# A pooled input half by seven products behind the state-space branch, and half the pooled parts kept on chip

## The chip, the cores and the metric

The kernel runs on one core of a Trainium2 chip, as one launch. The metric is device time in microseconds (us), taken over repeated runs; lower is better. The engines are named as in the profile: PE is TensorE (matmuls), PEld its weight loads, DVE is VectorE, ACT is ScalarE, POOL is GpSimd, SP is SyncE. SP issues the weight loads; POOL issues the transfers spoken of here.

## The reference

One layer of a decoder trunk on 512 tokens of width 1024, in float32. After a modulated RMS norm, one input product gives the inputs of three branches and three gates. The branches are a state-space one (SSD), dilated attention, and pooling over four windows:

```python
    for gi, w in enumerate(POOL_WINDOWS):        # 2, 4, 8, 16
        csg = cs[:, :, gi]
        shifted = jnp.pad(csg, ((0, 0), (w, 0), (0, 0)))[:, :S]
        count = jnp.minimum(t + 1, w).astype(jnp.float32)[None, :, None]
        outs.append((csg - shifted) / count - ug[:, :, gi])
    pooled = jnp.stack(outs, axis=2)
    return jnp.einsum('bsgi,gio->bsgo', pooled, w_mix).reshape(b, S, POOL_WIDTH)
...
    y_pool = (_multi_scale_pool(u.astype(f32), w_pool_mix) * pool_scale).astype(dtype) @ w_pool_out
...
    return (g_ssd * y_ssd + g_attn * y_attn + g_pool * y_pool) @ w_out
```

`u` has 1024 channels in four groups of 256, one for each window, and `w_mix` is one 256 x 256 matrix for each group. Behind the output product come a residual, a second modulated norm, and a feed-forward layer (1024 to 4096 with a squared ReLU, and back).

## The kernel before, in words

**Data.** Activations lie with the channels on the 128 partitions and the 512 tokens along a row, in blocks of 128 x 512. Blocks come from one pool of numbered slots: `blk(name)` takes a free slot, `free` gives it back, and the next taker waits until all that read or wrote the slot has ended. Eight PSUM banks work alike (`acc`, `psm`).

**Products.** A float32 product is made of three matmuls (`mm3`, L304 to L307): each operand is split into a high part (rounded) and a low part (the rest), and high x low, high x high and low x high are added up in PSUM. `gemm_feat` (L309) makes a half (512 outputs) as four banks, over 8 rows of weights; that is 96 matmuls of 512 columns. The weights come through `wstream` (L291), two rows at a time: SP loads `raw`, ACT makes the high part `wh` (a cast, L288), DVE the low part `wl` (L288). In the mode `st["adds"]`, ACT makes minus the high part (L281) and a DMA issued by POOL adds the weights from DRAM to it (L282), so that DVE has nothing to do for the weights. Three `wh` and three `wl` tiles are in turn, so a cast waits for the matmuls that used the tile three steps before.

**Seven products.** `seven_products` (L781) makes the same half by Strassen's scheme: seven products of quarter size in place of eight, with sums of quarters of the weights (`wsum`, made on DVE, L808 to L811) and of the input (`tx`, `ty`, made once by `input_sums`, L763, and used by all later calls). These are 168 matmuls of 256 columns (L826); their casts stand at L801 and L802, and the results are put together on DVE (L838).

**Branches.** The pooled branch: `pool(half)` makes four blocks of `u`, then on DVE the window sums (copies of 1 to 8 columns and adds of the shifted block, L1131 and L1132), the edge factors (L1136), the mean less `u` (L1137), and splits the result into `pdh` and `pdl` (L333). `pool_mix(gi)` multiplies one group by its matrix: two banks of 6 matmuls, each evacuated by ACT (L1167, high part) and DVE (L1168, low part) into two of eight staging blocks; a DMA on POOL (L1172) stores each part in DRAM. Later `again` (L1292) loads all 16 parts back.

**Order.** The program's text gives the order, and a scheduler arranges instructions by priority within it. `call` puts work on a side list, and after each pair of weight rows `tick` (L261) issues the next entry of it behind that pair's casts. Around the change the order before was: U's first half, U's second half (from here in the mode `adds`), the first gate of the state-space branch (GS 0) with the mixing of all four groups and the four pieces of the input sums on the side list, the first projection of that branch, GS 1 by seven products (the mode `adds` off), the second projection; then the reloads, the first pooled gate (GP 0) by seven products, its projection (which reads the pooled parts), GP 1, its projection, the output product.

**Output section.** The output product's second half is made in halves of 256 tokens (`out_block`, L1349, `ta` and `tb`), so that sums over tokens of squares (`sum_tokens`, L1366) and the second norm's factor (`spread`, L216) can be made for the first half while the second is still multiplied; `ff_rows` does the first feed-forward block by halves as well.

## Time and profile before

| what | value |
|---|---|
| time, median of 3 runs | 1091.45 us (1090.39 to 1092.57) |
| the profiled execution's own time | 1090.45 us |
| span of its trace | 1088.7 us |
| granted TensorE clock, mean | 1.0 |
| PE / DVE / ACT / POOL busy, share of the span | 99% / 69% / 50% / 4% |
| DMA, mean over the span | 137 GB/s |

The profiled execution lies 1.0 us under the median of the runs. The span goes from its first instruction to its last, and the time has 1.75 us around it. In a row of a timeline the first number is the start, the second the duration of one row, `x2` means two instructions in a row, and the bracket tells how long the engine was idle before and what ended that. Matmuls are pipelined: a 512-column matmul shows 0.39 us, and the next starts earlier than that, so prices are read from start to start. The same holds for DVE, whose durations overlap by some 0.08 us.

### The profile page before, as it was taken

The numbers are of one execution on the slowest core, as the hardware profiler recorded it, in microseconds if no ns is written. First come the engines' busy times: TensorE is split into PE (matmuls) and PEld (weight loads), VectorE is DVE, ScalarE is ACT, GpSimd is POOL, SyncE is SP. The second block draws the span as 40 slices with busy tenths as digits, with TensorE's granted clock in tenths as the row PEclk, the third lists the DMA queues.
The fourth block names the chain that finished last, engine by engine and source line by source line (L and its number), as shares of the span: only waits on it lengthen the run. The fifth ranks groups of instructions, "written<-read, shape, count | busy, mean of one in ns | idle before, by whom it ended". The sixth has DMA issues, their size and how long they took to land.

```text
span 1088.7 us, 15639 instructions
## 1 busy us (share of the span) xinstructions
PE 1081.3 (99%) x6022; PEld 934.0 (86%) x6022; DVE 748.1 (69%) x1429; ACT 547.6 (50%) x889; POOL 39.8 (4%) x70
## 2 busy tenths in 40 slices
PE   8999999999999999999999999999999999999998
PEld 7878888888887888888879989899889989989987
DVE  8955746684677966567966556667878587587664
ACT  8965874543444943757554335354434334335330
POOL 0000000000000010001311100000000000000000
PEclk9999999999999999999999999999999999999999
DMA  9723143546555243247956534450215224134032
GB/s 352 298 97 92 64 162 121 194 155 200 176 179 152 98 137 114 78 116 176 266 178 203 142 120 141 132 211 1 97 39 156 80 75 145 60 106 137 20 116 78
DMA packets 50958, 148.71 MB, mean 137 GB/s; under 512 B 6066, under 2 KB 6834, under 8 KB 50884
## 3 DMA queue, kind: packets, MB, share of 16 engines
q1 hardware_dynamic: 43088, 126.08, 34.7%
q0 software_dynamic: 7072, 20.45, 7.6%
q8 instruction: 47, 0.77, 0.3%
q10 hardware_dynamic: 724, 1.18, 0.3%
q14 instruction: 27, 0.22, 0.1%
HBM read 141.37 MB, written 6.32 MB: 136 GB/s over the span
## 4 chain that ended last, share of the span: by engine, by line
PE 96%; DVE 2%; DMA 1%; ACT 1%; issue 1%; SPq 0%; DVEq 0%; ACTq 0%
PE psacc L305 22%; PE psacc L307 22%; PE psacc L306 22%; PE psacc L826 17%; PE psacc L545 4%; PE psS L624 1%; PE psy L1087 1%; PE pso L740 1%; PE psyo L1095 1%; PE pso L738 1%; DMA rawl<-in_w_in_dram 1%; PE psqT L603 0%; PE pskT L608 0%; PE psst L1046 0%; PE pspT L721 0%
## 5 line engine op out<-in xcount | busy, mean ns | idle before, releaser
L288 DVE TENSOR_TENSOR wl<-raw,wh 128x1024 fp32r<-128x1024 f32 x116 | 141.6, 1222 | 126.1 <-ACT wh L288 116.4
L288 ACT CAST wh<-raw 128x1024 fp32r<-128x1024 f32 x116 | 121.5, 1049 | 185.6 <-PE psacc L306 105.6
L305 PE MATMUL psacc<-hl,wh 128*128 128x512 f32 x320 | 128.8, 403 | 0.2 <-ACT pT L722 0.2
L307 PE MATMUL psacc<-hh,wl 128*128 128x512 f32 x320 | 124.7, 390 | 0.0
L306 PE MATMUL psacc<-hh,wh 128*128 128x512 f32 x320 | 124.6, 389 | 0.0
L306 PE MATMUL psacc<-ah,wh 128*128 128x512 f32 (+1 forms) x260 | 100.4, 386 | 0.0
L305 PE MATMUL psacc<-al,wh 128*128 128x512 f32 (+1 forms) x260 | 100.4, 386 | 0.0
L307 PE MATMUL psacc<-ah,wl 128*128 128x512 f32 (+1 forms) x260 | 100.3, 386 | 0.0
L305 PE MATMUL psacc<-wl,rh 128*128 128x512 f32 x192 | 77.4, 403 | 0.0
L307 PE MATMUL psacc<-wh,rl 128*128 128x512 f32 x192 | 75.2, 392 | 0.0
L306 PE MATMUL psacc<-wh,rh 128*128 128x512 f32 x192 | 75.1, 391 | 0.0
L305 PEld LDWEIGHTS psacc<-hl,wh 128*128 128x128 f32 x320 | 60.1, 188 | 13.4 <-issue 1.2
L306 PEld LDWEIGHTS psacc<-hh,wh 128*128 128x128 f32 x320 | 60.2, 188 | 13.3 <-issue 1.4
L307 PEld LDWEIGHTS psacc<-hh,wl 128*128 128x128 f32 x320 | 60.0, 188 | 12.9
L1470 DVE SCALAR_TENSOR_TENSOR xr<-psacc,modv,xr 128x512 f32<-128x512 f32 (+1 forms) x65 | 44.7, 739 | 20.4 <-PE psacc L307 20.4
L802 DVE TENSOR_TENSOR wl<-rawl,wh 128x512 fp32r<-128x512 f32 (+1 forms) x36 | 33.6, 954 | 35.4 <-ACT wh L801 35.3
L307 PEld LDWEIGHTS psacc<-ah,wl 128*128 128x128 f32 x260 | 48.8, 188 | 9.8
L305 PEld LDWEIGHTS psacc<-al,wh 128*128 128x128 f32 x260 | 48.9, 188 | 9.7
L306 PEld LDWEIGHTS psacc<-ah,wh 128*128 128x128 f32 x260 | 48.9, 188 | 9.6
L801 ACT CAST wh<-wsum 128x1024 fp32r<-128x1024 f32 x18 | 19.0, 1054 | 75.7 <-PE psacc L306 73.8
L801 ACT CAST wh<-rawl 128x512 fp32r<-128x512 f32 (+1 forms) x36 | 29.1, 833 | 49.8 <-PE psacc L306 25.1
L305 PEld LDWEIGHTS psacc<-wl,rh 128*128 128x128 f32 x192 | 36.1, 188 | 7.7 <-ACT qT L604 0.5
(426 smaller groups left out, 2777.9 us busy)
## 6 DMA issues: line engine op xcount, KB each, us to landing
raw<-in_w_in_dram SPq DMA_DIRECT2D x74, 512.0 KB, 3.6
raw<-in_w_ff_dram SPq DMA_DIRECT2D x52, 512.0 KB, 3.7
wa<-in_w_ada_dram SPq DMA_DIRECT2D x64, 256.0 KB, 3.4
wada<-in_w_ada_dram SPq DMA_DIRECT2D x14, 512.0 KB, 7.9
rawl<-in_w_ff_dram SPq DMA_DIRECT2D x12, 512.0 KB, 3.5
wst<-in_w_in_dram SPq DMA_DIRECT2D x16, 256.0 KB, 7.9
M<-prow POOLq DMA_DIRECT2D x16, 256.0 KB, 3.7
wl<-in_w_in_dram POOLq DMA_DIRECT2D x8, 512.0 KB, 5.5
```

What stands on the lines that cost most here:

```text
L288: edges[:] = S.copy(wh, raw), V.tensor_tensor(wl, raw, wh.bitcast(F32), ALU.subtract)
L305: mm(ps, lhsT=wh, rhs=xl, start=first, stop=False)
L306: mm(ps, lhsT=wh, rhs=xh, start=False, stop=False)
L307: mm(ps, lhsT=wl, rhs=xh, start=False, stop=last)
L545: mm(ps[j], lhsT=t[:, j, :], rhs=w, start=first, stop=last)
L624: mm(so[b], lhsT=qT[:, b * P : (b + 1) * P], rhs=kT[:, (b + 1) * P - n : (b + 1) * P], start=True, stop=True)
L738: mm(od, lhsT=vs[kb][:, hs], rhs=pT[b // 2][:, cs : cs + P], start=(b == 0), stop=False, skip_group_check=True)
L740: mm(ov[:, b, :], lhsT=vs[b][:, hs], rhs=pT[0][:, b * P : (b + 1) * P], start=False, stop=(gi == 2 and b == 3), skip_group_check=True)
L801: S.copy(h, x)
L802: V.tensor_tensor(l, x, h.bitcast(F32), ALU.subtract)
L826: mm(o, lhsT=x[:, cs], rhs=y, start=first and k == 0 and j == 0 and n == 0, stop=k == 3 and n == 2, skip_group_check=True)
L1470: V.scalar_tensor_tensor(xT[d][:, ts], p[:, : ts.stop - ts.start], modv[:, 3, d : d + 1], xT[d][:, ts], ALU.mult, ALU.add)
```

## The change

The order becomes: U's first half as before; GS 0 (now the first in the mode `adds`) and the first state-space projection with the mixing of groups 0 and 1 on the side list, and the input sums issued behind the gate's last evacuation; GS 1 by seven products; the second projection; **then U's second half, by seven products**; GP 0 by seven products with the mixing of groups 2 and 3 on its side list; the reloads; the pooled projections with GP 1 between them. Only groups 0 and 1 go to DRAM and back (8 stores, 8 reloads); groups 2 and 3 are written straight into blocks that the projection reads. The matrices of groups 2 and 3 are split into ordinary blocks. The eight staging blocks are given back after group 1.

In the output section the first block is made for all 512 tokens at once, the sums over tokens and the norm's factor are issued amid a later block's matmuls, and the first feed-forward block does rows 0 to 4 by halves and rows 5 to 7 for all tokens, into the same four banks; its squared ReLU then takes 512 columns at once.

```diff
@@ -1120,8 +1120,7 @@
             yl.append(l)
 
 
-    def pool(half):
-        us = evac(gemm_feat(w_in, 8, U + half, hh, hl), "u")
+    def pool(half, us):
         for j in range(4):
             gi = 2 * half + j // 2
             u = us[j]
@@ -1141,17 +1140,22 @@
             dh.append(x)
             dl.append(y)
 
-    mixw, stage = [], []
+    mixw, mixp, stage = [], [], []
 
     def mix_weights(n):
 
         raw = raws.tile([P, 2, T], F32, tag="raw", name=uid("wmix"))
         for i in range(2):
             nc.sync.dma_start(raw[:, i, :].rearrange("p (k c) -> p k c", k=2), a["w_pool_mix"][2 * n + i])
-        wh, wl = (exp.tile([P, 2, T], F32R, tag=f"{x}{n}", name=uid("wm" + x)) for x in "LN")
-        S.copy(wh, raw)
-        V.tensor_tensor(wl, raw, wh.bitcast(F32), ALU.subtract)
-        mixw.extend([t[:, i, :].rearrange("p (k c) -> p k c", k=2) for t in (wh, wl)] for i in range(2))
+        if n == 0:
+            wh, wl = (exp.tile([P, 2, T], F32R, tag=f"{x}{n}", name=uid("wm" + x)) for x in "LN")
+            S.copy(wh, raw)
+            V.tensor_tensor(wl, raw, wh.bitcast(F32), ALU.subtract)
+            parts = [(wh[:, i, :], wl[:, i, :]) for i in range(2)]
+        else:
+            parts = [split(raw[:, i, :], "wm") for i in range(2)]
+            mixp.extend(parts)
+        mixw.extend([t.rearrange("p (k c) -> p k c", k=2) for t in p] for p in parts)
 
     def pool_mix(gi):
         wh, wl = mixw[gi]
@@ -1163,15 +1167,21 @@
             cs = slice(m * P, (m + 1) * P)
             for k in range(2):
                 mm3(ps, wh[:, k, cs], wl[:, k, cs], dh[2 * gi + k], dl[2 * gi + k], k == 0, k == 1)
-            x, y = stage[4 * (gi % 2) + 2 * m : 4 * (gi % 2) + 2 * m + 2]
+            if gi < 2:
+                x, y = stage[4 * gi + 2 * m : 4 * gi + 2 * m + 2]
+            else:
+                x, y = blk("poolh", F32R), blk("pooll", F32R)
             S.activation(x, ps, AF.Copy, scale=vc("pool_scale", gi * 2 + m))
             V.scalar_tensor_tensor(y, ps, vc("pool_scale", gi * 2 + m), x.bitcast(F32), ALU.mult, ALU.subtract)
             free(ps)
             for t, l in ((x, ph_), (y, pl_)):
-                l.append(dp.tile([P, T], F32, name=uid("pool")))
-                nc.gpsimd.dma_start(l[-1], t.bitcast(F32))
-        if gi == 3:
+                l.append(t if gi > 1 else dp.tile([P, T], F32, name=uid("pool")))
+                if gi < 2:
+                    nc.gpsimd.dma_start(l[-1], t.bitcast(F32))
+        if gi == 1:
             free(*stage)
+        elif gi > 1:
+            free(*mixp[gi - 2])
         free(*dh[2 * gi : 2 * gi + 2], *dl[2 * gi : 2 * gi + 2])
 
 
@@ -1208,6 +1218,14 @@
 
     def take_z(g):
         return evac(gemm_feat(w_in, 8, Z + g, hh, hl), "z", AF.Silu)
+
+    def behind_evac(f):
+
+        def go():
+            with tc.issue_after(st["evac"].ins):
+                f()
+
+        return go
 
     def rest(n):
         side.extend([lambda: None] * n)
@@ -1270,32 +1288,31 @@
     show("oT", [h.bitcast(F32) for h in oh + ol])
     tq, sums = input_sums(hh, hl)
 
-    pool(0)
+    pool(0, evac(gemm_feat(w_in, 8, U, hh, hl), "u"))
     call(mix_weights, 0)
     st["adds"] = True
-    pool(1)
+    sg = gate(GS, 0)
     call(pool_mix, 0)
-    side.append(lambda: (mix_weights(1), pool_mix(1)))
-    call(pool_mix, 2)
-    call(pool_mix, 3)
-    side.extend(sums)
-    sg = gate(GS, 0)
+    call(pool_mix, 1)
+    side.extend(behind_evac(f) for f in sums)
     project(a["w_ssd_out"], 8, 0, yh, yl, sg)
     flush()
     st["adds"] = False
     sg = gate(GS, 1, tq)
     project(a["w_ssd_out"], 8, 1, yh, yl, sg)
-
-    def again(l, name):
-        for i, d in enumerate(l):
-            l[i] = blk(name, F32R)
+    pool(1, seven_products(w_in, U + 1, hh, hl, tq))
+    call(mix_weights, 1)
+    call(pool_mix, 2)
+    call(pool_mix, 3)
+    sg = gate(GP, 0, tq)
+    flush()
+    for l, name in ((ph_, "poolh"), (pl_, "pooll")):
+        for i in range(4):
+            d, l[i] = l[i], blk(name, F32R)
             nc.gpsimd.dma_start(l[i], d)
-
-    again(ph_, "poolh")
-    again(pl_, "pooll")
-    for ch in range(2):
-        sg = gate(GP, ch, tq, ch == 1)
-        project(a["w_pool_out"], 8, ch, ph_, pl_, sg, last=True)
+    project(a["w_pool_out"], 8, 0, ph_, pl_, sg, last=True)
+    sg = gate(GP, 1, tq, True)
+    project(a["w_pool_out"], 8, 1, ph_, pl_, sg, last=True)
     flush()
     assert not background
     show("mixed", [h.bitcast(F32) for h in mh + ml])
@@ ...
-        for j in range(4):
+        both = slice(0, T)
+        residual(both, 0, out_block(both, 0))
+        for j in range(1, 4):
             sq = residual(ta, j, out_block(ta, j))
...
+        ps = out_block(tb, 1, 3, lambda: rs.append(scale(sum_tokens(ta, sq))))
         residual(tb, 1, ps)
+        ps = out_block(tb, 2, 5, lambda: rs.append(spread(rs[0], 2, "r2")))
...
+        ff_rows(ta, (0,))
         sp = sum_tokens(tb, sq)
...
+        ff_rows(ta, (3, 4))
...
+        ff_rows(tb, range(5))
...
+        ff_rows(both, range(5, 8))
...
-    square_relu(0, [[(ffa[j], ta), (ffb[j], tb)] for j in range(4)])
+    square_relu(0, [[(ff[j], full)] for j in range(4)])
```

In the rows of order below, a name's number tells tiles of one name apart. First VectorE at the start of GS 1. Before, all input sums (`tx`, `ty`, from `tq`) are made when the weights of the first products (`wl`, L802) come:

```order
L333 TENSOR_TENSOR txl_5298<-tq_5154,txh_5297 128x512
L333 TENSOR_TENSOR tyl_5302<-tq_5155,tyh_5301 128x512
L802 TENSOR_TENSOR wl_5322<-rawl_5313,wh_5321 128x512
L802 TENSOR_TENSOR wl_5322<-rawl_5317,wh_5321 128x512
L811 TENSOR_TENSOR rawl_5313<-raw_5314,wsum_5327 128x2x256
L811 TENSOR_TENSOR rawl_5317<-raw_5318,wsum_5332 128x2x256
L802 TENSOR_TENSOR wl_5370<-raw_5314,wh_5369 128x512
L802 TENSOR_TENSOR wl_5370<-raw_5318,wh_5369 128x512
L907 TENSOR_TENSOR sg_5109<-psacc_5117,sg_5109 128x512
L907 TENSOR_TENSOR sg_5110<-psacc_5118,sg_5110 128x512
L914 TENSOR_TENSOR sg_3936<-sg_3936,sg_5109 128x512
L907 TENSOR_TENSOR sg_5111<-psacc_5119,sg_5111 128x512
```

Now the last pooled low part to be stored (`pool_4838`, L1175) stands just ahead, and the input sums of later pieces stand between it and the weights; `txl_5031` and `tyl_5035` take staging blocks that hold stored parts:

```order
L1175 SCALAR_TENSOR_TENSOR pool_4838<-psmix_4909,vec_79,pool_4837 128x512
L767 TENSOR_TENSOR tq_4953<-hh_249,hl_257 128x512
L333 TENSOR_TENSOR txl_5031<-tq_4955,txh_5030 128x512
L768 TENSOR_TENSOR tq_4954<-hh_253,hl_261 128x512
L808 TENSOR_TENSOR wsum_5066<-rawl_5052,raw_5053 128x2x256
L333 TENSOR_TENSOR tyl_5035<-tq_4956,tyh_5034 128x512
L802 TENSOR_TENSOR wl_5061<-rawl_5052,wh_5060 128x512
L809 TENSOR_TENSOR rawl_5052<-rawl_5052 128x2x256
L810 TENSOR_TENSOR wsum_5066<-wsum_5066,rawl_5052 128x2x256
L802 TENSOR_TENSOR wl_5109<-raw_5053,wh_5108 128x512
L811 TENSOR_TENSOR rawl_5052<-raw_5053,wsum_5066 128x2x256
L802 TENSOR_TENSOR wl_5109<-raw_5057,wh_5108 128x512
```

The projection's evacuations (L907) and the weights `wl_5142` of the first sum of weight quarters follow, at the 16th row from `tyl_5035` on. What moved is the stores' end: it now stands ahead of the weights of the first products.

Next VectorE in GP 0. Before, it has the weights (L802, L288) and the results (L838) of the products alone:

```order
L802 TENSOR_TENSOR wl_5874<-rawl_5724,wh_5873 128x1024
L802 TENSOR_TENSOR wl_5902<-rawl_5728,wh_5901 128x1024
L838 TENSOR_TENSOR r_5836<-psacc_5846,keep_5774 128x256
L838 TENSOR_TENSOR r_5837<-psacc_5846,keep_5774 128x256
L802 TENSOR_TENSOR wl_5936<-raw_5725,wh_5935 128x512
L802 TENSOR_TENSOR wl_5936<-raw_5729,wh_5935 128x512
L288 TENSOR_TENSOR wl_5978<-raw_5975,wh_5977 128x1024
L838 TENSOR_TENSOR r_5838<-keep_5917,keep_5820 128x256
L838 TENSOR_TENSOR r_5839<-keep_5917,keep_5820 128x256
L838 TENSOR_TENSOR r_5836<-psacc_5749,keep_5834 128x256
L838 TENSOR_TENSOR r_5837<-psacc_5749,keep_5834 128x256
```

Now the windows of U's second half (`win`, L1130 to L1136, out of the results `r`) stand between the weights:

```order
L1130 COPY win_5704<-r_5545 128x1
L1130 COPY win_5695<-win_5692 128x4
L1136 SCALAR_TENSOR_TENSOR win_5680<-win_5680,r_5543 128x512
L1131 TENSOR_TENSOR win_5695<-win_5692 128x508
L1131 TENSOR_TENSOR win_5704<-r_5545 128x511
L333 TENSOR_TENSOR pdl_5686<-win_5680,pdh_5685 128x512
L1135 TENSOR_TENSOR win_5695<-win_5695,cst 128x7
L1130 COPY win_5707<-win_5704 128x2
L1131 TENSOR_TENSOR win_5707<-win_5704 128x510
L802 TENSOR_TENSOR wl_5923<-rawl_5740,wh_5922 128x1024
L802 TENSOR_TENSOR wl_5973<-rawl_5744,wh_5972 128x1024
L802 TENSOR_TENSOR wl_6007<-raw_5741,wh_6006 128x512
```

Both U's stage and this one are by seven products, so that windows, weights and results share VectorE there; before, the windows stood in the stage whose weights a DMA completed.

Last TensorE at the end of GP 0, where the pooled projection (`psacc_5971` before, `psacc_6058` now) begins. Before:

```order
L826 MATMUL psacc_5748<-tyh_5301,wl_5936 128x256
L826 MATMUL psacc_5748<-tyl_5302,wh_5935 128x256
L826 MATMUL psacc_5748<-tyh_5301,wh_5935 128x256
L826 MATMUL psacc_5748<-tyh_5301,wl_5936 128x256
L305 MATMUL psacc_5971<-pooll_5708,wh_5977 128x512
L306 MATMUL psacc_5971<-poolh_5692,wh_5977 128x512
L307 MATMUL psacc_5971<-poolh_5692,wl_5978 128x512
```

Now the mixing of the last group (`psmix`, from `pdl_5737` and `pdh_5736`) ends six matmuls ahead of it:

```order
L305 MATMUL psmix_5961<-pdl_5737,wmh_5827 128x512
L306 MATMUL psmix_5961<-pdh_5736,wmh_5827 128x512
L307 MATMUL psmix_5961<-pdh_5736,wml_5828 128x512
L826 MATMUL psacc_5764<-tyl_5049,wh_6006 128x256
L826 MATMUL psacc_5764<-tyh_5048,wh_6006 128x256
L826 MATMUL psacc_5764<-tyh_5048,wl_6007 128x256
L826 MATMUL psacc_5764<-tyl_5049,wh_6006 128x256
L826 MATMUL psacc_5764<-tyh_5048,wh_6006 128x256
L826 MATMUL psacc_5764<-tyh_5048,wl_6007 128x256
L305 MATMUL psacc_6058<-pooll_6050,wh_6064 128x512
L306 MATMUL psacc_6058<-poolh_6042,wh_6064 128x512
L307 MATMUL psacc_6058<-poolh_6042,wl_6065 128x512
```

The reload `pooll_6050`, which the projection's first matmul reads, now takes the block of the mixing matrix's high part `wmh_5827`, whose last reader is the second row here. Before, no row of the pooled branch stands in this stage, and the reloads are issued from the second state-space projection on.

More of the change, by code (lines that the diff above doesn't have):

```diff
@@ L1352, in out_block @@
                 wh, wl = wres[k]
-                mm3(ps[:, :hw], wh[:, cs], wl[:, cs], mh[k][:, ts], ml[k][:, ts], k == 0, k == 7)
+                mm3(ps[:, : ts.stop - ts.start], wh[:, cs], wl[:, cs], mh[k][:, ts], ml[k][:, ts], k == 0, k == 7)
+                if k == at:
+                    amid()
             return ps
@@ L1357, in residual @@
             d = 4 + j
-            V.scalar_tensor_tensor(xT[d][:, ts], ps[:, :hw], modv[:, 0, d : d + 1], xT[d][:, ts], ALU.mult, ALU.add)
+            V.scalar_tensor_tensor(xT[d][:, ts], ps[:, : ts.stop - ts.start], modv[:, 0, d : d + 1], xT[d][:, ts], ALU.mult, ALU.add)
             free(ps)
-            sq = half_tile()
+            sq = tmp[0] if ts.stop - ts.start == T else half_tile()
             S.activation(sq, xT[d][:, ts], AF.Square)
@@ L1375, in high2 @@
         def high2(ts, rp, k):
-            u = us[k] = half_tile()
+            u = us[ts.start, k] = half_tile()
             V.scalar_tensor_tensor(u, xT[k][:, ts], A2[:, k : k + 1], rp[:, :hw], ALU.mult, ALU.mult)
@@ L1380, in low2, with norm2, ff_rows @@
         def low2(ts, k):
-            V.scalar_tensor_tensor(gl[k][:, ts], us.pop(k), modv[:, 1, k : k + 1], gh[k][:, ts].bitcast(F32), ALU.add, ALU.subtract)
-        def norm2(ts, rp, k):
-            if k < 8:
+            V.scalar_tensor_tensor(gl[k][:, ts], us.pop((ts.start, k)), modv[:, 1, k : k + 1], gh[k][:, ts].bitcast(F32), ALU.add, ALU.subtract)
+        late = []
+        def norm2(ts, rp, ks):
+            for k in ks:
                 high2(ts, rp, k)
-            if k > 0:
-                low2(ts, k - 1)
-        def ff_rows(ts, ps, ks):
+                late.append((ts, k))
+                if len(late) > 1:
+                    low2(*late.pop(0))
+        def ff_rows(ts, ks):
             for k in ks:
@@ L1392, in ff_rows @@
                 for j in range(4):
-                    cs = slice(j * P, (j + 1) * P)
-                    mm3(ps[j][:, :hw], wh[:, cs], wl[:, cs], gh[k][:, ts], gl[k][:, ts], k == 0, k == 7)
+                    o, cs = ff[j][:, ts], slice(j * P, (j + 1) * P)
+                    for n, (x, y) in enumerate(((wh, gl), (wh, gh), (wl, gh))):
+                        mm(o, lhsT=x[:, cs], rhs=y[k][:, ts], start=k == 0 and n == 0 and ts.start == 0, stop=k == 7 and n == 2, skip_group_check=True)
         def scale(sp):
```

49 lines of the change are left out of this document (21 added, 28 removed).

## The prediction

> **What bounds the kernel now.** I read the page first: where the span goes by engine, and the chain that ended last.
>
> ```profile
> span 1088.7 us, 15639 instructions
> PE 1081.3 (99%) x6022; PEld 934.0 (86%) x6022; DVE 748.1 (69%) x1429; ACT 547.6 (50%) x889; POOL 39.8 (4%) x70
> PE 96%; DVE 2%; DMA 1%; ACT 1%; issue 1%; SPq 0%; DVEq 0%; ACTq 0%
> ```
>
> TensorE is busy for 99% of the span and makes 96% of the chain. So a change gains by taking matmuls out, and loses by anything that makes TensorE wait. The list of TensorE's waits has one place near the change:
>
> ```profile
> PE psacc L305 <- DVE pool L1168: 0.8, 1, 0.8
> ```
>
> Then the stages from the second input half to the first pooled gate, as a table of stretches: the U half and the gate of the state-space branch to 548.4 (with the last pooled parts mixed behind it), the rest of the first state-space projection to 569.9, its second gate by seven products to 590.1, the second projection to 612.0, the first pooled gate by seven products to 634.
>
> ```profile
> core 0: us, PE busy (x) PEld busy (x) DVE busy (x) ACT busy (x) POOL busy (x), PEclk, DMA share, GB/s
> 514.50:548.40 33.90, 33.90 (x152) 28.06 (x151) 29.96 (x68) 21.03 (x29) 10.03 (x16) 1.00 0.90 256
> 548.40:569.90 21.50, 20.68 (x91) 16.76 (x90) 15.76 (x28) 8.84 (x15) 3.96 (x6) 1.00 0.59 167
> 569.90:590.10 20.20, 20.20 (x168) 20.04 (x168) 13.74 (x20) 10.63 (x14) 2.67 (x5) 1.00 0.47 155
> 612.00:634.00 22.00, 22.00 (x177) 21.55 (x176) 15.01 (x23) 12.21 (x19) 2.11 (x4) 1.00 0.62 182
> ```
>
> VectorE is the engine to watch. A seven-product stage of 20 us already has 13.7 to 15.0 us of VectorE work, where the old place of the pooled windows had the accumulating DMAs take the low halves of the weights off VectorE. The prices of matmuls are start to start, from TensorE's timeline:
>
> ```profile
> 549.07 0.39 PE L305 MATMUL psacc<-ynl,wh 128*128 128x512 f32 x1
> 549.29 0.39 PE L306 MATMUL psacc<-ynh,wh 128*128 128x512 f32 x1
> 550.50 0.50 PE L305 MATMUL psacc<-ynl,wh 128*128 128x512 f32 x1 [0.82 <-DVE pool L1168]
> 570.07 0.28 PE L826 MATMUL psacc<-hh,wh 128*128 128x256 f32 x1
> 570.18 0.28 PE L826 MATMUL psacc<-hh,wl 128*128 128x256 f32 x1
> ```
>
> One of 512 columns takes 0.227 us (three make 0.68), one of 256 takes 0.12 us (168 of them fill the 20.2 us of the stage in the table).
>
> **Matmuls saved.** U's second half was 96 matmuls of 512 columns, 96 x 0.227 = 21.8 us. As seven products it is 168 of 256 columns, 168 x 0.12 = 20.2 us: -1.6 us. In the output and first feed-forward section, 24 + 36 pairs of 256-column matmuls become single ones of 512 columns; each saves 2 x 0.12 - 0.227 = 0.013 us: -0.8 us. There the first sum over tokens now follows its last square after 12 matmuls, not 24. The cover is read here:
>
> ```profile
> 729.41 0.28 PE L307 MATMUL psacc<-mxh,wrl 128*128 128x256 f32 x1
> 729.73 0.48 DVE L1358 SCALAR_TENSOR_TENSOR xr<-psacc,modv,xr 128x256 f32<-128x256 f32 x1 [0.79 <-PE psacc L307]
> 730.25 0.42 ACT L1361 ACTIVATE crow<-xr 128x256 f32<-128x256 f32 x1 [1.76 <-DVE xr L1358]
> 732.41 0.28 PE L1369 MATMUL psr<-ones,sums 128*128 128x1 f32 x2
> ```
>
> The block's last matmul starts at 729.41 and its square is done at 730.67: 1.3 us later. Twelve matmuls are 1.44 us, so it just fits: between -0.8 and, if the margin fails at both sums, +0.2; I take -0.8.
>
> **The old stall.** The 0.82 us wait at 550.50 (a gap of 1.21 where 0.23 is due, so 0.98 us) came from pooled parts whose high and low halves held up the projection. In the new order no pooled part of the last two groups is mixed there: -1.0 us (0 if the first two take its place). Savings together: -3.4 us.
>
> **First new wait: the stores and the input sums.** The eight blocks that pooled parts are staged in are given back after the second group, and the input sums of pieces 1 to 3 (`tx`, `ty`) get them next. So VectorE and ScalarE wait for the stores to DRAM to land, and everything behind them on these engines waits too. The line of the stores shows how long that is, and that it already happened before, but with time to spare:
>
> ```profile
> L1172 POOL DMA_DIRECT2D pool<-pool x16: 539/560/893, 524.1 to 551.8; - x16
>   ACT tyh L332: 2.6, 1
>   DVE txl L333: 2.1, 1
> DMA to landing us min/median/max: 3.4/6.6/10.1
> ```
>
> From the second group's last matmul to the second gate's first, 48 matmuls of 512 columns stand (10.9 us), and the weights of its third product (`wl_5142`, in VectorE's rows under the change) are due another 48 x 0.12 = 5.8 us later: 16.7 us. The last stores but one go out about 0.8 us after that group's end (the multiply-subtract), land at 7.4, and from the block that waits for them VectorE has 16 instructions to the end of that `wl`, about 9.4 us at the prices below: 16.8 us. That is level at the median, and each further microsecond of a store is one of stall: 0 to 10.1 - 6.6 = 3.5 us. Four stores stand in one queue within two microseconds, so I take +1.5.
>
> The Trainium skill ("DMA: Bandwidth & Descriptors", Anatomy of one DMA) prices a DMA issued by GpSimd at about 2.0 us plus its bytes over 436 GB/s; for 256 KB that is 2.6 us, and the term would be 0. The trace has 3.4 at the least and 6.6 at the median for these stores, and the trace decides.
>
> **Second new wait: VectorE over U's and the pooled gate's products.** First the price of an instruction when VectorE has no idle time, start to start:
>
> ```profile
> 514.39 0.14 DVE L1131 COPY win<-u 128x1 f32<-128x1 f32 x1
> 514.46 0.68 DVE L1132 TENSOR_TENSOR win<-u 128x511 f32<-128x511 f32 x1
> 515.05 0.14 DVE L1131 COPY win<-u 128x1 f32<-128x1 f32 x1
> ```
>
> 0.60 us for 512 columns, 0.07 for a small copy. The seven-product stage before, on VectorE:
>
> ```profile
> 610.23 1.37 DVE L907 TENSOR_TENSOR r<-psacc,r 128x512 f32<-128x512 f32 x2 [1.32 <-PE psacc L307]
> 611.51 0.68 DVE L914 TENSOR_TENSOR sg<-sg,r 128x512 f32<-128x512 f32 x1
> 612.12 1.28 DVE L907 TENSOR_TENSOR r<-psacc,r 128x512 f32<-128x512 f32 x2
> 613.31 1.21 DVE L802 TENSOR_TENSOR wl<-wsum,wh 128x1024 fp32r<-128x1024 f32 x1
> 614.45 1.28 DVE L914 TENSOR_TENSOR sg<-sg,r 128x512 f32<-128x512 f32 x2
> 619.39 1.23 DVE L802 TENSOR_TENSOR wl<-rawl,wh 128x1024 fp32r<-128x1024 f32 x1 [1.82 <-ACT wh L801]
> 622.03 1.22 DVE L802 TENSOR_TENSOR wl<-rawl,wh 128x1024 fp32r<-128x1024 f32 x1 [1.42 <-ACT wh L801]
> 623.95 0.76 DVE L838 TENSOR_TENSOR r<-psacc,keep 128x256 f32<-128x256 f32 x2 [0.70 <-PE psacc L826]
> 624.62 1.28 DVE L802 TENSOR_TENSOR wl<-raw,wh 128x512 fp32r<-128x512 f32 x2
> 627.79 1.23 DVE L288 TENSOR_TENSOR wl<-raw,wh 128x1024 fp32r<-128x1024 f32 x1 [1.88 <-ACT wh L288]
> ```
>
> 1.14 us for 1024 columns (613.31 to 614.45), 0.34 for 256 (two in 623.95 to 624.62). In the new order VectorE has, from the second state-space projection's first evacuation to the last `pdl` of the pooled windows, 51 instructions of about 512 columns, 9 of 1024, 12 of 256 and 18 small ones: 30.6 + 10.3 + 4.1 + 1.3 = 46.2 us. It can't start before that projection's result: 1.8 us ahead of the next stage's first matmul (610.23 against 612.0). In U's stage it must sit idle as it did here, 1.82 + 1.42 = 3.2 us, for `wh` casts that wait for TensorE itself. So the last `pdl` is done -1.8 + 46.2 + 3.2 = 47.6 us after U's first matmul. TensorE gets to the matmul that reads it after 168 + 162 of 256 columns and 18 of 512: 330 x 0.12 + 18 x 0.227 = 43.7 us. The wait is 4 us at least; with the further 1.88 us of idle time for a cast and 0.7 for an evacuation, as in the last and the 623.95 row, 6.6 at most. Part of those will be filled, since VectorE is late: I take +5.5.
>
> **Third new wait: the last reload.** The pooled parts of the first two groups come back to blocks that are free late. The one that the first matmul of the pooled projection reads, `pooll_6050`, takes the block of the mixing matrix's high part, so it can be issued only when the last group's last matmul but one is done. Then follow one of 512 columns and six of 256, 0.95 us, and the projection. The price of a reload:
>
> ```profile
> poolh<-pool POOLq DMA_DIRECT2D x8, 256.0 KB, 3.5
> pooll<-pool POOLq DMA_DIRECT2D x8, 256.0 KB, 3.2
> ```
>
> 3.2 - 0.95 = 2.3 us, or with 3.5 and 0.53 us of issue (539 ns at the least in the row of the stores) 3.1: I take +2.6. Nothing covers it, and it adds to the wait ahead of it, since it starts when that ends. By the skill's 2.6 us for a DMA it would be 1.7.
>
> Sum: -3.4 + 1.5 + 5.5 + 2.6 = +6.2 us on the profiled execution, 1090.45 to 1096.65. That execution is 1.0 us under the median of the runs, 1091.45, so the forecast is 1097.6 us. With the three waits at their low ends (0, 4.0, 2.3) the sum is +2.9, 1094.4; at their high ends (3.5, 6.6, 3.1) +9.8, 1101.3. A difference under 0.2%, 2.2 us, is no difference here.
>
> **The rivals.** *VectorE keeps ahead* (not slower). If the instructions pack closer than 0.60 us, or TensorE reaches U's stage later than VectorE needs, the second wait goes. It decides at 47.6 - 43.7 = 4 us, 9% of VectorE's work in these stages. Then -3.4 + 0 + 2.6, or about 1090.7. For it: the profile's VectorE is 69% busy over all. Against it: every price above is from a stretch without idle time, and each engine goes in order. Chance 0.09.
>
> *All three hide* (faster). If the blocks come free early enough, the saved matmuls and the old stall remain: 1091.45 - 3.4 = 1088.0. It needs reloads landing within 0.95 us, or issued from another block than the order shows; no row has that. Chance 0.07.
>
> *The queue backs up* (slower still). GpSimd issues accumulating DMAs of the weights, stores and reloads in one order; if a store of the second group lands at 10.1 us and the rest behind it likewise, TensorE's wait at the second gate is 3.5 us for each of its two late products (`wl_5142`, and the last input sum, read later): 7.0 instead of 1.5, so 1097.6 + 5.5 = 1103.1. Decides from 7.4 us of landing on. For it: the DMA share of 0.90 in the first stretch. Against: fewer stores now. Chance 0.14.
>
> **How the numbers follow.** The forecast has 0.70, the rivals 0.09, 0.07 and 0.14. Faster by over 0.2%: 0.07 for the second rival and 0.01 of the first; the same: 0.08; slower: 0.84. The range leaves out the second rival and the upper part of the last: from 1090.7 to 1103.0.
>
> **What would show it.** Right: the group of pooled mixing in the pooled gate's stage shows TensorE waiting for VectorE at `pdl` (L333), 4 to 7 us together; the first matmul of the pooled projection waits 2 to 3 us for a DMA of `pooll`; VectorE has nearly no idle time in the 20 us ahead; at the second gate's start a wait of up to 3.5 us for L802 or L333. Wrong: TensorE without gaps in these three places, or a loss that sits in the output section instead.

## The result, and the profile after

The changed kernel takes 1098.4 us in the median of 5 runs (1097.15 to 1101.71), the kernel before 1091.45 us; the ratio is 1.0062 with a 95% interval of 1.0041 to 1.0083. It is slower by 0.6%, and the forecast was 1097.6 us. The profiled execution is the slowest of the five, 1101.71 us, 11.3 us over that of before; so its trace shows more loss than the median has.

The page of the changed kernel: TensorE is still at 99%, and its share of the chain falls by a point, to VectorE.

```profile
span 1099.9 us, 15642 instructions
PE 1085.4 (99%) x6034; PEld 937.9 (85%) x6034; DVE 762.6 (69%) x1452; ACT 548.2 (50%) x889; POOL 27.6 (3%) x50
PE 95%; DVE 3%; ACT 1%; DMA 1%; issue 0%; SPq 0%; DVEq 0%; ACTq 0%
```

TensorE's waits (us in total, times, longest): the old wait for the pooled part is gone, and three new ones are there.

```profile
PE psacc L826 <- ACT keep L831: 4.9, 3, 3.2
PE psacc L305 <- DMA pooll<-pool: 2.5, 1, 2.5
PE psacc L826 <- DVE txl L333: 0.9, 1, 0.9
```

In TensorE's timeline they look like this. The spacing behind the waits is to be read as well.

```profile
554.20 0.39 PE L826 MATMUL psacc<-txl,wh 128*128 128x256 f32 x1 [0.86 <-DVE txl L333]
...
620.05 0.28 PE L826 MATMUL psacc<-hh,wh 128*128 128x256 f32 x1
620.17 0.28 PE L826 MATMUL psacc<-hh,wl 128*128 128x256 f32 x1
623.64 0.41 PE L826 MATMUL psacc<-hl,wh 128*128 128x256 f32 x1 [3.19 <-ACT keep L831]
623.87 0.40 PE L826 MATMUL psacc<-hh,wh 128*128 128x256 f32 x1
...
635.87 0.39 PE L826 MATMUL psacc<-tyl,wh 128*128 128x256 f32 x1 [1.50 <-ACT keep L831]
...
642.85 0.50 PE L305 MATMUL psacc<-pooll,wh 128*128 128x512 f32 x1 [2.47 <-DMA pooll<-pool]
643.18 0.39 PE L306 MATMUL psacc<-poolh,wh 128*128 128x512 f32 x1
...
645.17 0.63 PE L307 MATMUL psacc<-poolh,wl 128*128 128x512 f32 x1
645.60 0.63 PE L305 MATMUL psacc<-pooll,wh 128*128 128x512 f32 x1
```

Two things are to be seen. The waits stand at the second state-space gate, in the pooled gate's stage and at the first matmul of the pooled projection. And behind two of them matmuls come at nearly half rate: 0.21 us apart from 623.64 to 627.3 (0.12 is due), and 0.43 apart (645.17 to 645.60, 0.227 due) from 644.3 to 647.7. The table of stretches has that as the granted clock (the column ahead of the DMA share): 1.00 in the wait itself, then 0.54 and 0.51. Its first row is the pooled gate's stage as a whole, with VectorE busy for 27.17 of 28.9 us, 94%.

```profile
core 0: us, PE busy (x) PEld busy (x) DVE busy (x) ACT busy (x) POOL busy (x), PEclk, DMA share, GB/s
611.30:640.20 28.90, 24.04 (x162) 22.37 (x160) 27.17 (x60) 14.70 (x23) 3.12 (x6) 0.94 0.54 173
...
620.00:623.60 3.60, 0.45 (x4) 0.24 (x3) 3.53 (x7) 1.73 (x4) 0.11 (x1) 1.00 0.76 245
623.60:627.10 3.50, 3.46 (x17) 3.46 (x18) 3.50 (x11) 0.51 (x1) 0.00 (x0) 0.54 0.99 355
...
644.30:647.80 3.50, 3.50 (x10) 2.71 (x10) 0.64 (x1) 0.00 (x0) 0.00 (x0) 0.51 0.37 138
```

Why a copy on ScalarE? The copies called `keep` take a product out of PSUM into a block. The rows of that tile tell what ScalarE sat idle for before them:

```profile
  PE psacc L826: 11.6, 24
  DVE win L1136: 4.9, 2
  DVE win L1131: 3.2, 1
```

Three copies waited for VectorE's window steps (`win`), though they read nothing of them. The reading that fits is the reuse of blocks: the block that a copy writes is one that such a step gives back. TensorE's waits of 0.17 and 3.19 us end with two of these copies. There TensorE waited for a PSUM bank, the bank for the copy, the copy for a block, and the block for VectorE.

The wait of 1.50 us at 635.87 is another case. ScalarE wasn't idle ahead of its copy. In ScalarE's order the copy stands behind a cast of weights, and that cast waited for TensorE's own matmuls:

```profile
634.29 1.04 ACT L288 CAST wh<-raw 128x1024 fp32r<-128x1024 f32 x1 [0.72 <-PE psacc L826]
635.24 0.58 ACT L831 COPY keep<-psacc 128x512 f32<-128x512 f32 x1
```

So this part of the waiting isn't shown to be VectorE's.

The sum over the two profiled executions, as gaps beyond the due spacing: matmuls saved -2.4 and the old stall -1.0; the three waits 1.0 + 5.3 (0.33, 3.35 and 1.66) + 2.6; half rate 1.6 + 1.6; in the first 50 us of the program, which the change doesn't touch, 2.0 (the granted clock is 0.97 there against 1.00 before); some 0.5 of slow starts behind the waits. That makes 11.2 of the 11.3 us. The 2.0 us in the first 50 are a stretch of half rate too (9.48 to 12.89 us), so this execution has three such stretches. Each lowers the mean granted clock by 0.0016, which gives the 0.995 on record for it; the other four executions have 0.997 or 0.998, which by this estimate is two stretches or one. The median execution has 0.997, one stretch less; that accounts for 1.6 to 2.0 of the 3.3 us by which this one lies above it.

### The profile page after: what moved, and what is told of

Read it like the earlier page. It is cut to its first block, busy times and chain, and to the rows that moved or that the text cites. A ratio compares the mean times of both kernels' runs of the same rounds, so it can differ in the third digit from the quotient of the medians.

```text
span 1099.9 us, 15642 instructions
## 1 busy us (share of the span) xinstructions
PE 1085.4 (99%) x6034; PEld 937.9 (85%) x6034; DVE 762.6 (69%) x1452; ACT 548.2 (50%) x889; POOL 27.6 (3%) x50
## 4 chain that ended last, share of the span: by engine, by line
PE 95%; DVE 3%; ACT 1%; DMA 1%; issue 0%; SPq 0%; DVEq 0%; ACTq 0%
PE psacc L305 21%; PE psacc L307 21%; PE psacc L306 21%; PE psacc L826 17%; PE psacc L545 3%; PE psacc L1419 2%; PE psS L624 1%; PE psy L1087 1%; DVE wl L802 1%; PE pso L740 1%; PE psyo L1095 1%; PE pso L738 1%; PE psqT L603 0%; PE pskT L608 0%; PE psst L1046 0%; PE pspT L721 0%
## 5 line engine op out<-in xcount | busy, mean ns | idle before, releaser
L288 DVE TENSOR_TENSOR wl<-raw,wh 128x1024 fp32r<-128x1024 f32 x116 | 141.7, 1223 | 131.5 <-ACT wh L288 121.8
L288 ACT CAST wh<-raw 128x1024 fp32r<-128x1024 f32 x116 | 121.6, 1049 | 191.5 <-PE psacc L306 113.2
L305 PE MATMUL psacc<-hl,wh 128*128 128x512 f32 x288 | 116.3, 404 | 0.2 <-ACT pT L722 0.2
L307 PE MATMUL psacc<-hh,wl 128*128 128x512 f32 x288 | 112.2, 390 | 0.0
L306 PE MATMUL psacc<-hh,wh 128*128 128x512 f32 x288 | 112.2, 389 | 0.0
L305 PEld LDWEIGHTS psacc<-hl,wh 128*128 128x128 f32 x288 | 54.1, 188 | 12.2 <-issue 1.2
L306 PEld LDWEIGHTS psacc<-hh,wh 128*128 128x128 f32 x288 | 54.2, 188 | 12.1 <-issue 1.4
L307 PEld LDWEIGHTS psacc<-hh,wl 128*128 128x128 f32 x288 | 54.1, 188 | 11.6
L802 DVE TENSOR_TENSOR wl<-rawl,wh 128x512 fp32r<-128x512 f32 (+1 forms) x40 | 37.4, 955 | 34.4 <-ACT wh L801 34.4
L801 ACT CAST wh<-rawl 128x512 fp32r<-128x512 f32 (+1 forms) x40 | 32.5, 833 | 48.8 <-PE psacc L306 24.4
L826 PE MATMUL psacc<-txl,wh 128*128 128x256 f32 x160 | 46.3, 290 | 1.0 <-DVE txl L333 0.9
```

The costliest lines, as they stand in the source:

```text
L288: edges[:] = S.copy(wh, raw), V.tensor_tensor(wl, raw, wh.bitcast(F32), ALU.subtract)
L305: mm(ps, lhsT=wh, rhs=xl, start=first, stop=False)
L306: mm(ps, lhsT=wh, rhs=xh, start=False, stop=False)
L307: mm(ps, lhsT=wl, rhs=xh, start=False, stop=last)
L801: S.copy(h, x)
L802: V.tensor_tensor(l, x, h.bitcast(F32), ALU.subtract)
```

## The experiments

### The output section alone

The kernel before with the output section of the change, and nothing else of it:

```diff
-        for j in range(4):
+        residual(both, 0, out_block(both, 0))
+        for j in range(1, 4):
             sq = residual(ta, j, out_block(ta, j))
...
+        ff_rows(both, range(5, 8))
```

> The kernel before with the output section of the change alone (first block for all tokens, sums and factor amid a block, rows 5 to 7 for all tokens). Theory: 60 pairs of 256-column matmuls become 512-column ones, 60 x 0.013 = 0.8 us less, no new wait: 1090.6 us. Rival: the sum over tokens comes before its square is done, and the saving is eaten by waits at the two sums: 1091.5 us or a little above, with a wait of TensorE at the sums over tokens.

Measured: 1089.96 us beside 1090.99 for the kernel before in the same series, a ratio of 0.9995 (0.9978 to 1.0011). TensorE's waits stay as they were before, with none at a sum over tokens:

```profile
PE psacc L305 <- DVE pool L1168: 0.9, 1, 0.9
PE psrx L477 <- DVE diag L474: 0.3, 1, 0.3
```

So no new wait comes from this part, and the loss is not there. A saving of 0.8 us fits the medians, but the interval doesn't show it. The traces do: from the first matmul of the output product to the last that reads `tyl` in the feed-forward part, TensorE takes 343.75 us here and 344.72 in the kernel before, 0.97 less (343.77 in the changed kernel).

### Reloads in the order of their use

```diff
-    for l, name in ((ph_, "poolh"), (pl_, "pooll")):
-        for i in range(4):
+    for i in range(4):
+        for l, name in ((ph_, "poolh"), (pl_, "pooll")):
```

> The changed kernel, reloads asked for by pairs of high and low part, so that the blocks of the first two rows are the ones that come free first and the late blocks go to the last two rows, which the projection reads 36 to 72 matmuls later. Theory: the wait of 2.5 us for the reload goes, and with it the half-rate stretch of some 3.4 us (1.7 us lost) that followed it in the changed kernel's trace: 1098.4 - 2.6 - 1.7 = 1094.1 us. Rival (the projection is held by its weights or by the last group's parts as well): the wait turns up at the next row, and less than 1 us is gained, 1097.5 us or more.

Measured: 1093.85 us, ratio to the kernel before 1.0027 (1.0016 to 1.0038). TensorE's waits:

```profile
PE psacc L826 <- ACT keep L831: 3.2, 1, 3.2
...
PE psacc L306 <- DMA poolh<-pool: 0.2, 1, 0.2
```

The wait for the reload falls from 2.5 to 0.2 us, and there is no half rate behind it. The gain is 4.5 us on the medians, against 4.3 expected. The third wait was as priced. The wait of 1.5 us for `keep` doesn't show here either, though ScalarE has the same cast and the same copy in the same order (631.21 and 632.17): TensorE has seven matmuls of the projection to do meanwhile (631.13 to 633.25), for which the reloads have landed. So a part of the gain is that wait. The wait of 3.2 us, and the half rate behind it (15 matmuls from 621.4 on, 1.4 us), are still there.

### Shorter windows

The doubling steps of the second half stop after the first, so the results of groups 2 and 3 are those of window 2 (this kernel leaves the rest of the windows out):

```diff
-            while d < WINDOWS[gi]:
+            while d < (WINDOWS[gi] if half == 0 else 2):
```

> The changed kernel, the second half's windows stopped after one doubling step (the results of groups 2 and 3 are those of window 2): 20 VectorE instructions fewer in the pooled gate's stage, 10 x 0.67 = 6.7 us of its work. Theory (VectorE is late in that stage, and ScalarE's copies of results, named keep, wait for blocks that the window steps give back late): both long waits for keep go, 5.2 us, and the half-rate stretch behind the first, 1.6 us: 1091.6 us, with the wait for the reload still there. Rival (the blocks are short whatever VectorE does, or the casts of weights are the limit): the waits for keep stay over 3 us, 1095 us or more.

Measured: 1089.1 us, ratio 0.9981 (0.9972 to 0.999). No `keep` is left among the waits, and the granted clock stays at 1.00 through the stage, in which VectorE is busy for 80% now:

```profile
PE psacc L305 <- DMA pooll<-pool: 0.8, 1, 0.8
PE psacc L826 <- DVE txl L333: 0.6, 1, 0.6
```

```profile
611.50:640.00 28.50, 27.65 (x177) 24.95 (x176) 22.91 (x40) 16.56 (x25) 4.26 (x8) 1.00 0.71 220
```

The waits for copies go with VectorE's load, as the theory had it. The time is 2.5 us under the expected one. The wait for the reload fell too, from 2.5 to 0.8 us, and the half rate behind it is gone (1.6 us); together that is 3.3 us. This kernel is the faster one, but it leaves work out.

### Four blocks more, the same load

The low halves of the second half's window results are made in place and not used; the mixing of groups 2 and 3 reads the high half twice:

```diff
-            x, y = split(cur, "pd")
+            if half == 0:
+                x, y = split(cur, "pd")
+            else:
+                x = y = blk("pdh", F32R)
+                S.copy(x, cur)
+                V.tensor_tensor(cur, cur, x.bitcast(F32), ALU.subtract)
```

> The changed kernel, with the low halves of the second half's four window results made in place and not used (the mixing of groups 2 and 3 reads the high half twice), so that four blocks less are taken while VectorE has the same instructions. Theory (VectorE is late, and the copies named keep only pass that on): the waits stay between 3 and 6 us together, at copies or at the mixing, 1096.5 to 1099 us. Rival (four more blocks free the copies, and lateness at the mixing is under 1 us): 1098.4 - 5.2 - 1.6 = 1091.6 to 1093 us.

Measured: 1100.17 us, ratio 1.0072 (1.0046 to 1.0098). The waits for copies are gone, and one wait of 5.65 us for the window results stands at the mixing. TensorE's timeline:

```profile
623.68 0.28 PE L826 MATMUL psacc<-hh,wl 128*128 128x256 f32 x1
629.62 0.80 PE L305 MATMUL psmix<-pdh,wmh 128*128 128x512 f32 x1 [5.65 <-ACT pdh L1142]
```

This is what tells the two causes apart. With blocks to spare the wait doesn't go, it moves to the mixing, which the prediction had named (though to its first matmul, not to the last `pdl`), and is of about the same size (5.7 against 5.3 us, of which 1.7 were the cast's). The blocks decide where TensorE stands while VectorE works. The time is 1.2 us above the upper end of what was expected; the wait for the reload, 2.45 us, is still there, with half rate behind both waits.

### The second pooled gate ahead of the first projection

```diff
+    sg = gate(GP, 0, tq)
     call(mix_weights, 1)
     call(pool_mix, 2)
     call(pool_mix, 3)
-    sg = gate(GP, 0, tq)
+    sg1 = gate(GP, 1, tq, True)
     flush()
```

The reloads and the two projections follow.

> The changed kernel with the second pooled gate ahead of the first pooled projection, and the last two groups mixed in that gate: VectorE has the windows done 20 us before anyone waits, and the reloads take the blocks of input sums that the last gate gives back 15 us ahead. Theory (lateness of VectorE and of the reloads is the whole loss): 1098.4 - 5.2 - 2.6 - 3.3 = 1087.3 us, no wait over 1 us but the one at the state-space gate. Rival (the copies keep still wait for blocks of the windows in the first pooled gate's stage, since all blocks are in use): 2 to 5 us of waits and a half-rate stretch remain there, 1091 to 1095 us.

Measured: 1092.61 us, ratio 1.0009 (0.9993 to 1.0025): 5.8 us less than the changed kernel, no difference from the kernel before. The waits are small and many, and now for weights:

```profile
PE psacc L826 <- DVE wl L802: 1.4, 2, 0.8
...
PE psacc L826 <- ACT wh L801: 0.9, 1, 0.9
PE psacc L826 <- DVE txl L333: 0.8, 1, 0.8
PE psacc L826 <- ACT keep L831: 0.4, 1, 0.4
```

```profile
612.00:632.00 20.00, 17.20 (x133) 16.04 (x133) 19.22 (x37) 10.03 (x15) 0.00 (x0) 1.00 0.30 106
```

The time is the rival's, though not by the rival's mechanism: of the copies 0.4 us is left, and the three waits for weights come from VectorE again, busy for 19.22 of 20 us, which is now late with the next gate's weights (ScalarE sat idle for 3.43 us before the cast `wh`, until VectorE had made a sum of weights). Three stages by seven products in a row leave no place for some 14 us of windows (an estimate: 22 instructions at 0.60 us and 18 at 0.07). The reload's wait is gone.

### The pooled gate by a plain product

With the reloads in order of use, and the weights' low halves completed by DMA in that stage:

```diff
+    st["adds"] = True
-    sg = gate(GP, 0, tq)
+    sg = gate(GP, 0)
+    st["adds"] = False
```

> The changed kernel with the reloads by pairs, and its first pooled gate as a plain product of 96 matmuls in the mode in which a DMA completes the low halves of the weights, so that VectorE has the windows of that stage to itself. Theory (VectorE's load in that stage makes the waits): TensorE has 21.8 us of matmuls for 20.2 there, +1.6, and no wait over 0.5 us at copies, mixing or reload, no half-rate stretch: from the kernel with the reloads by pairs, 1093.85 - 3.4 - 1.6 + 1.6 = 1090.4 us, about the kernel before or up to 1 us under it. Rival (the window chain itself, or the accumulating DMAs, hold the mixing): a wait of 2 us or more at the mixing, 1093 us or more.

Measured: 1096.49 us, ratio 1.0043 (1.0029 to 1.0058). Neither copies nor mixing are waited for, but there is a new wait at the stage's start:

```profile
PE psacc L307 <- DMA wl<-in_w_in_dram: 3.3, 1, 3.3
```

```profile
601.47 0.90 POOL L282 DMA_DIRECT2D wl<-in_w_in_dram  x1 [65.51 <-ACT wl L281]
604.36 0.88 POOL L282 DMA_DIRECT2D wl<-in_w_in_dram  x1 [1.99 <-DVE win L1131]
607.64 0.86 POOL L282 DMA_DIRECT2D wl<-in_w_in_dram  x1 [2.40 <-ACT wl L281]
```

The first of the stage's accumulating DMAs is issued at 601.47, and TensorE goes on at 608.68. Half rate is here too, 2.3 us lost. The theory holds in that VectorE's waits go, and fails in the time, which is 6.1 us above the expected 1090.4: the mode needs a lead that this place doesn't give.

### Window steps on GpSimd

The copies and adds of one block (of two in the second kernel), with the reloads in order of use:

```diff
+                E = nc.gpsimd if half == 1 and j in (1,) else V
-                V.tensor_copy(nx[:, :d], cur[:, :d])
-                V.tensor_tensor(nx[:, d:], cur[:, d:], cur[:, : T - d], ALU.add)
+                E.tensor_copy(nx[:, :d], cur[:, :d])
+                E.tensor_tensor(nx[:, d:], cur[:, d:], cur[:, : T - d], ALU.add)
```

> The changed kernel with the reloads by pairs, and the doubling steps of one block's windows (the second block of group 2, three copies and three adds) on GpSimd: 3 x 0.67 = 2.0 us less for VectorE ahead of the steps for which ScalarE's copies wait. Theory (that wait, 3.2 us, follows VectorE's load one for one): about 1.2 us of it remain and no half-rate stretch: 1093.85 - 2.0 - 1.5 = 1090.3 us. Rival (GpSimd takes longer for its steps than VectorE saves, or slows VectorE while both work): VectorE waits for GpSimd, the wait stays at 3 us or more, 1093.5 us or above.

> As the kernel with one block's windows on GpSimd, but two blocks (also the first of group 3, four copies and four adds), 4.7 us less for VectorE. Theory: no wait at the copies, no half rate: 1093.85 - 3.4 - 1.5 = 1089.0 us. Rival (GpSimd's two chains, 14 instructions one after the other, end later than VectorE would have): a wait of 2 us or more at the copies or the mixing, 1092 us or above.

Measured: 1100.17 us (ratio 1.007, 1.005 to 1.0089) and 1100.22 us (1.0073, 1.0057 to 1.009). Both are slower by 6 us than the kernel without that edit. GpSimd's and VectorE's timelines of the first of them:

```profile
608.53 1.95 POOL L1132 TENSOR_TENSOR win<-r 128x511 f32<-128x511 f32 x1 [7.33 <-DVE r L838]
611.04 1.49 POOL L1132 TENSOR_TENSOR win<-win 128x510 f32<-128x510 f32 x1
```

```profile
609.56 1.47 DVE L1132 TENSOR_TENSOR win<-r 128x511 f32<-128x511 f32 x1
610.95 2.12 DVE L802 TENSOR_TENSOR wl<-raw,wh 128x512 fp32r<-128x512 f32 x2
612.99 0.16 DVE L1131 COPY win<-win 128x2 f32<-128x2 f32 x1
613.06 0.68 DVE L1132 TENSOR_TENSOR win<-win 128x510 f32<-128x510 f32 x1
614.67 0.17 DVE L1136 TENSOR_TENSOR win<-win,cst 128x7 f32<-128x7 f32 x1 [0.93 <-POOL win L1132]
```

The rival is right, in both of its ways. An add takes GpSimd 1.49 to 1.95 us, where VectorE takes 0.68; VectorE's own add at 609.56, while GpSimd adds, takes 1.47; and VectorE then waits for the chain. TensorE's wait at the copies is 2.9 us in the first kernel, and 3.0 and 2.8 in the second. More of the reloads' waits come back as well, since the mixing is later (2.8 and 1.8 us in the first of the two).

### Waits made on purpose

The kernel before, with instructions on VectorE that leave the values as they are, ahead of each of the two sums over tokens (9 and 17 in the first kernel, 14 and 25 in the second). Here the first of the two places in the first kernel:

```diff
+        for _ in range(9):
+            V.tensor_tensor(sq, sq, sq, ALU.max)
         ps = out_block(tb, 0)
         r = scale(sum_tokens(ta, sq))
```

> The kernel before with 9 and 17 VectorE instructions of 256 columns (the larger of a square and itself) ahead of the two sums over tokens in the output section. At 0.34 us each they make TensorE wait about 1.5 us at the first sum and 2.8 us at the second. Theory (a stretch of half rate of 3.4 us follows when a wait takes up more than about half of one of the windows in which activity is counted): none behind the first wait, perhaps one behind the second. Rival (the half rate in the changed kernel is chance and not due to the waits): none behind either.

> As the kernel with short waits, but 14 and 25 instructions: TensorE waits about 3.2 us at the first sum and 5.5 us at the second. Theory: a stretch of 3.4 us in which matmuls of 256 columns stand 0.21 us apart, not 0.12, starts behind each wait or within 2 us of its end, 1.5 to 1.7 us lost each time. Rival: the spacing stays at 0.12 us.

Measured, one execution each: 1101.59 and 1110.86 us. The waits were longer than planned: 2.2 and 6.0 us in the first kernel, 4.5 and 9.7 us in the second. The granted clock behind them, of the first kernel (behind 2.2 us and behind 6.0 us):

```profile
734.60:738.00 3.40, 3.25 (x27) 3.25 (x28) 1.53 (x8) 0.68 (x2) 0.00 (x0) 1.00 0.00 0
...
755.00:758.50 3.50, 3.26 (x15) 3.26 (x16) 3.06 (x13) 1.17 (x3) 0.00 (x0) 0.50 0.00 0
758.50:762.00 3.50, 3.50 (x21) 3.50 (x21) 0.20 (x1) 0.00 (x0) 0.00 (x0) 0.58 0.00 0
```

and of the second kernel, behind 4.5 us:

```profile
737.00:740.40 3.40, 3.29 (x15) 3.29 (x16) 1.17 (x7) 0.47 (x2) 0.00 (x0) 0.50 0.00 0
```

No half rate follows 2.2 us; it follows 4.5, 6.0 and 9.7 us. So it comes from the waits and not by chance. In the other traces of this study, waits of up to 1.8 us within the program were followed by none, and of eleven waits of 2.4 to 5.7 us ten were followed by one. The one without it (2.95 us) is in the kernel with two windows on GpSimd, so the length of a wait alone doesn't decide it.

What does can be read from the granted clock in slices of 0.1 us. Between the first 15 us and the last matmul, half rate lasts 3.41 us in six places of these traces, and two, three or four times that in six others (6.83, 10.24 and 13.65 us), each of which begins while TensorE waits. For the two kernels with added waits 3.4 us were expected each time, with 1.5 to 1.7 us lost; it was 6.83, 10.24 and 13.65 us, with 2.0 to 2.2 us lost in the matmuls behind the wait. In the changed kernel's trace half rate begins at 9.48, 623.88 and 644.36 us, which are 180 and 6 times 3.413 us apart. So one can lay a grid of 3.41 us over a trace, through the places where half rate begins, and read how long TensorE was busy in each field. Here a field of the changed kernel with the one behind it, and two of the kernel with two windows on GpSimd, in which its wait of 2.95 us lies (columns as above):

```profile
640.95:644.36 3.41, 1.51 (x7) 1.25 (x8) 3.41 (x6) 1.99 (x5) 0.38 (x1) 1.00 0.99 245
644.36:647.77 3.41, 3.41 (x10) 2.67 (x9) 0.58 (x1) 0.00 (x0) 0.00 (x0) 0.50 0.36 139
```

```profile
611.68:615.09 3.41, 1.69 (x14) 1.48 (x13) 3.41 (x7) 0.00 (x0) 3.41 (x5) 1.00 0.00 0
615.09:618.50 3.41, 2.18 (x18) 2.19 (x19) 3.41 (x6) 0.58 (x1) 3.41 (x4) 1.00 0.00 0
```

Behind each of the twelve full-rate fields in which TensorE was busy for 1.51 us or less, half rate begins; behind none with 1.69 us or more does it. A wait of 2.95 us that two fields share was not enough, and one of 2.47 us, of which 1.90 lie in one field, was. The fields lie otherwise against the program in each execution: counted back, the first one begins at about 0.3 us in the kernel with the short waits and at about 2.5 in the one with the long waits (an estimate from 751.20 and 736.41, where half rate begins there), though the two programs are the same up to the first sum. So a wait near 2 or 3 us may or may not be followed by half rate.

## Why the prediction was right

**Direction and size** were right, and the cause in the main: the three waits came in the three stages that the prediction had named.

**Matmuls saved** (-2.4 us) and **the old stall** (-1.0): the stall is absent from the waits after; the saved matmuls of the output section were tried alone, with 0.97 us less in the trace, where 0.8 was priced, and an interval of the medians that includes no change; those of U's second half weren't tried alone.

**First wait** (+1.5, between 0 and 3.5): 0.9 us of waiting, 1.0 with its gap, at an input sum and not at `wl_5142`. In other kernels of this study with the same rows in that place the gap is between 0.06 and 0.95 us. That the stores make it was not tried separately; what the trace of the changed kernel shows is VectorE idle for 3.30 us and ScalarE for 4.53 until a store lands, and from there to the late input sum VectorE busy for 22.17 of 22.2 us (532.0 to 554.2). The stores landed in 4.7 us at the median, not in the 6.6 that were priced; with 4.7 the prediction's own working gives no wait (0.8 + 4.7 + 9.4 is under 16.7). So that the term was near is luck, and what makes this wait stays open.

**Second wait** (+5.5, between 4 and 6.6): 5.3 us. Its cause, VectorE's load, holds for 3.7 of them; two experiments say so (shorter windows, four blocks more), and the gates first fit it. The other 1.7 us are the copy behind a cast on ScalarE, which the prediction didn't have; that the sum is so close to 5.5 is in part luck. The run with four blocks more measures VectorE's lateness without it, 5.65 us in one wait. The place was wrong: the prediction had TensorE reach the mixing and wait for `pdl` there. It waited earlier, for copies whose blocks, by the reading above, came from the window steps. The step that failed is the one that took the waiting instruction to be a reader of VectorE's result; the reuse of blocks made ScalarE another one.

**Third wait** (+2.6, between 2.3 and 3.1): 2.5 us of waiting, 2.6 with its gap, at the matmul and for the tile named. Asked for in the order of use, it went, and 4.5 us with it.

**What was left out:** the half rate, 3.2 us in the profiled execution. The prediction took a wait to cost its own length. The Trainium skill has this ("TensorE: Matmul & The Clock Gate", Part 1: The HAM clock gate): the clock falls to half after a window of about 3.4 us without activity, and the window isn't tied to the program. The trace agrees on the half rate (granted 0.50), on about 3.4 us of it (623.88 to 627.29, 644.36 to 647.77) and on windows that aren't tied to the program (0.3 and 2.5 us above); it differs on what sets it off, since waits of 2.5 and 3.2 us, shorter than that window, were enough.

So the forecast is close to the median in part because errors cancel: the half rate was missing, the first wait was priced 0.5 us too high, and the median execution loses less than the profiled one. On the profiled execution the prediction had 1096.65 us, and it took 1101.71. How the median's 7 us divide can't be read, since only the slowest execution has a trace.

**The rivals.** *VectorE keeps ahead* failed in the changed kernel, and came true when its load was cut. (Its sum leaves the first wait's 1.5 us out without a reason; with it, it would be 1092.2, not 1090.7.) *The queue backs up* failed: the wait for input sums stayed at 1 us. *All three hide* failed.

No kernel that computes the whole reference beat the kernel before beyond its interval: the output section alone has the lowest median, 1089.96 us.

## What to carry to other kernels

Where TensorE is at 99%, an edit that saves it 2 us is worth less than the place to which it moves another engine's work: add that engine's work up over the stage that it moves into, instruction by instruction, against the matmuls up to the first reader. With a fixed number of blocks handed on in order, look also at who takes the blocks that the late engine gives back, since that is who waits. A wait on TensorE of 2.5 us or more is to be priced with a likely half-rate stretch behind it, here 1.2 to 2.4 us more in the matmuls that follow; those of up to 2.2 us had none in any of these traces.

## What was not expected of the hardware

GpSimd's adds slow VectorE's: 1.47 us in place of 0.68 for 511 columns, and 2.12 in place of 1.29 for two subtractions of 512, while GpSimd takes 1.5 to 1.95 us for its own. Not each time: VectorE's add at 613.06 takes 0.68 us, with GpSimd's third one from 613.08 to 614.63. The Trainium skill names it ("GPSIMD Engine Reference", the table of specifications: GpSimd's interfaces to SBUF are shared with VectorE, with contention when VectorE has two inputs there), and the trace agrees for two of these three.

The start of the half rate isn't always the end of the wait: behind the reload it began 1.5 us after TensorE had gone on (642.85 and 644.36), and in the longer waits it began before TensorE went on (736.41, in the wait of 4.5 us that ended at 737.11).
